# A hybrid decoder layer on one core: the stretch from the output projection to the T4 operand in a written-down engine order, and the first gate/up pair regrouped

## The chip, the cores and the metric

The kernel runs on one core of a Trainium2 chip. The metric is the time of one execution on the device, in microseconds. Each core has five engines that run their own instruction streams in order: TensorE (PE, matmuls and transposes), VectorE (DVE), ScalarE (ACT), GpSimd (POOL) and SyncE (SP, which here issues most DMA transfers).

## The reference

One decoder layer, 1024 positions by 1024 channels, float32:

```python
h = rms_norm(x, mix_norm_g[l])
proj = jnp.einsum('bsd,de->bse', h, w_in[l])
...
mixed = jnp.concatenate([fox_out, diff_out], axis=-1)   # 8 FoX heads, 4 diff heads
x = x + jnp.einsum('bse,ed->bsd', mixed, w_out[l])
h = rms_norm(x, ffn_norm_g[l])
g = jnp.einsum('bsd,df->bsf', h, w_gate[l])             # 1024 x 2816
u = jnp.einsum('bsd,df->bsf', h, w_up[l])
x = x + jnp.einsum('bsf,fd->bsd', jax.nn.silu(g) * u, w_down[l])
return rms_norm(x, final_norm_g)
```

## The kernel before

**Matmuls.** Every float32 product is made of three: each operand is split into a high part (cast on ScalarE) and a low part (source minus high part, a subtract on VectorE or GpSimd), and hi·hi, hi·lo and lo·hi are summed in PSUM. A name ending in `h` or `l` in a row is such a part.

**The norm loop.** After attention, `for n, tb in enumerate(order)` goes through the eight row blocks of 128 positions in the order 7, 6, 5, 4, 0, 1, 2, 3. A round n makes, for each of the two column halves, 12 matmuls of the second half of the output projection (`pso`, L601; its operands `mx` come from the last attention groups, `mix` L501, `mx` L506 and L507) and a residual add on VectorE (`x`, L796); then the row norm: Square with a sum on ScalarE (L134), a scale on VectorE (`ss`, L135), a power of -1/2 on GpSimd (`ss`, L136), and the multiply `xn` on VectorE (L801).

**The operands.** From round 2 on, a round also transposes the block of two rounds ago (`pt`, L753) and cuts it into operands of a seven-product (Strassen-Winograd) scheme. The product names are "11", "21", "T1" to "T4" and "22"; each has a high and a low tile of 512 positions. `second_half(t)`, for blocks 4 to 7, makes "22" (`h22h`, `h22l`), the kept halves `r12` and `r22`, and the difference T3 (`st`, L765). `first_half(t)`, for blocks 0 to 3, makes "11", the difference T1 (`st`, L775), updates `r22` with it on GpSimd (`r`, L776), and T2. `first_half_below(t)` makes "21" and the difference T4 (`st`, L786). Differences go through small tiles `st` of one pool.

**The weights.** Gate and up weights arrive as raw quarter blocks (`raw`, L715, two buffers), on SyncE's queue. The sums that the scheme needs are made on GpSimd (`st`, L723). The weight operands are `oh` (ScalarE, L708) and `ol` (VectorE, L709). Four of them, `early`, are made before and during the norm loop; their products "22" and "T3" of gate and up are held in PSUM. `strassen_first` makes the other five products of both matrices for pair 0: gate's "11" and "21", up's "11" and "21", then the rest (matmuls `pst`, L825). It loads both weights and makes the sums s1 and s2 again. Ten more pairs follow in `strassen`, then the down projection.

**Who sets the order.** A scheduler that simulates the program sets the order on each engine in this stretch; in the attention part and in the last part it is partly written down already (`tc.manual_schedule`: the engines named run their instructions in program order).

Of the kernel before, what the change touches and what calls it, by code (L numbers as in the profile page):

```python
# [18 lines left out]
P = 128  # L19
# [52 lines left out]
def layer(ctx: ExitStack, tc: tile.TileContext, x, mix_g, w_in, b_forget, lq1, lk1, lq2, lk2,  # L72
# [543 lines left out]
    def xa_half(tb, nh):  # L616
        return xa[tb][:, nh * 512:nh * 512 + 512]
# [94 lines left out]
    def raw_w(m, q, c0, n):  # L712
        raw = wp.tile([P, 1056], F32, tag="wr", name="raw")
        v = raw[:, :4 * n].rearrange("p (k c) -> p k c", k=4)
        nc.sync.dma_start(out=v, in_=w_gu[m][:, 4 * q:4 * q + 4, c0:c0 + n])  # L715
        return v

    def small():
        return fa.tile([P, 4, P], F32, tag="st", name="st")

    def w_sum(op, x, y):
        t = small()
        G.tensor_tensor(t, x, y, op)  # L723
        return t

    def w_blocks(m, pair):
        q0, q1 = (raw_w(m, q, 2 * pair * P, 2 * P) for q in range(2))
        return q0[:, :, 0:P], q0[:, :, P:2 * P], q1[:, :, 0:P], q1[:, :, P:2 * P]

    def early_operands(m):  # L730

        a11, a21, a12, a22 = w_blocks(m, 0)
        s2 = w_sum(ALU.subtract, w_sum(ALU.add, a21, a22), a11)
        return operand(w_sum(ALU.subtract, a12, s2)), operand(w_sum(ALU.subtract, a11, a21))

    early = [early_operands(m) for m in range(2)]
# [4 lines left out]
    def split_at(name, c, src, le):  # L741
        h, l = (x[:, :, c:c + P] for x in b_op[name])
        A.copy(h, src)
        le.tensor_tensor(l, src, h.bitcast(F32), ALU.subtract)

    turn = [0]

    def transposed(t, q):
        pool, tag = ((ps_p, "pj"), (ps_t, "t"))[turn[0] % 2]
# [30 lines left out]
    def first_half_below(t):  # L780

        c = t % 4 * P
        pv = transposed(t, 1)
        split_at("21", c, pv, V)
        t4 = small()
        V.tensor_sub(t4, pv, r22[:, :, c:c + P])  # L786
        split_at("T4", c, t4, V)

    order = (7, 6, 5, 4, 0, 1, 2, 3)
    for n, tb in enumerate(order):  # L790
        xt = x2[tb // 2][:, tb % 2]
# [10 lines left out]
        if n == 2:  # L802
            b_op["22"] = big("h22h"), big("h22l")
        if n == 6:
            for name in ("11", "T1", "T2"):
                b_op[name] = tuple(big(name + c) for c in "hl")
        if n >= 2:
            t = order[n - 2]
            (second_half if t >= 4 else first_half)(t)
    for t in (2, 3):  # L810
        first_half(t)
    for name in ("21", "T4"):
        b_op[name] = tuple(big(name + c) for c in "hl")

# [12 lines left out]
        return ps  # L827

    product.n = 0
    held = []  # L830
    for m in range(2):
        held.append([product(a, name, ((ps_s, "s"), (ps_s, "s"), (ps_s, "s"), (ps_p, "pj"))[2 * m + k])
                     for k, (a, name) in enumerate(zip(early[m], ("22", "T3")))])
        for t in range(2):
            first_half_below(2 * m + t)
# [66 lines left out]

    def strassen_first(takes):

        rest = []
        for m, take in enumerate(takes):
            a11, a21, a12, a22 = w_blocks(m, 0)
            p1, u2, u3 = kept_tiles()
            A.copy(p1, product(operand(a11), "11"))
            s1 = w_sum(ALU.add, a21, a22)  # L910
            s2 = w_sum(ALU.subtract, s1, a11)

            def finish(take=take, p1=p1, u2=u2, u3=u3, p3=held[m][0], p7=held[m][1], s1=s1, s2=s2,
                       a22=a22):
                ps5 = product(operand(s1), "T1")
                ps = product(operand(s2), "T2")
                V.tensor_add(u2, ps, p1)
                V.tensor_add(u3, p7, u2)
                take(1, 1, ps5, u3)
                V.tensor_add(u2, ps5, u2)  # L920
                take(0, 1, p3, u2)
                take(1, 0, product(operand(a22), "T4"), u3)

            take(0, 0, product(operand(a12), "21"), p1)
            rest.append(finish)
        for finish in rest:
            finish()

    for pair in range(NF // 2):
        me = V if pair == NF // 2 - 1 else G  # L930
# [251 lines left out]
```

## Time and profile before

| | |
|---|---|
| runs | 1267.75, 1268.8, 1270.53 us; median 1268.8 |
| profiled execution | 1264.56 us, of which the span on the engines is 1262.9 us |
| TensorE in the span | 1223.7 us (97%), granted clock 0.99 of full speed |
| stretch in question | about 567 to 660 us |

The profile is of one execution, with times from the span's start. An engine's row in a timeline shows its start, its duration and, in brackets, how long the engine stood idle before it and what ended that. Rows of matmuls overlap (the next starts before the one before has drained), so the pace is read from starts.

### The profile page before, as it was taken

What the parts mean: (1) busy time and instruction counts of PE and PEld (TensorE: products, weight loads), DVE (VectorE), ACT (ScalarE), POOL (GpSimd) and SP (SyncE); (2) the same over time, 40 slices, a digit from 0 to 9 for tenths busy, and PEclk for the clock granted to TensorE, in tenths of its full rate; (3) what the DMA queues carried; (4) which work ended last, traced back from release to release, by engine and by line L of the source; (5) the groups of instructions that cost most, each with busy time, mean ns of one, the idle gap of its engine ahead of it and who ended that gap; (6) DMA issues with size and microseconds to landing.
All of it is one profiled execution on the core that took longest, in us unless ns stands there. A gap on an engine that the chain in (4) does not pass through costs nothing.

```text
span 1262.9 us, 18429 instructions
## 1 busy us (share of the span) xinstructions
PE 1223.7 (97%) x6341; PEld 1041.5 (82%) x6341; DVE 865.1 (69%) x1625; ACT 571.2 (45%) x1209; POOL 718.3 (57%) x657
## 2 busy tenths in 40 slices
PE   8999999999999998999799999999999999999997
PEld 8889988987898887888578888888888887788886
DVE  6556766757786788877777566566565568868765
ACT  4345545646685665545533332233332245434424
POOL 2322333134204363235768877777787758999973
PEclk9999999999999999999899999999999999999999
DMA  6231223031202144033223333323333357735313
GB/s 218 65 109 43 68 73 85 26 98 45 51 8 80 51 142 180 9 138 100 94 82 108 107 119 109 108 80 105 101 109 125 100 190 236 217 117 183 97 55 133
DMA packets 93374, 131.42 MB, mean 104 GB/s; under 512 B 7585, under 2 KB 56289, under 8 KB 93281
## 3 DMA queue, kind: packets, MB, share of 16 engines
q1 hardware_dynamic: 91440, 124.22, 30.8%
q10 hardware_dynamic: 1840, 6.03, 1.3%
q8 instruction: 50, 0.82, 0.3%
q14 instruction: 44, 0.35, 0.1%
HBM read 93.75 MB, written 30.18 MB: 98 GB/s over the span
## 4 chain that ended last, share of the span: by engine, by line
PE 82%; POOL 6%; DVE 4%; issue 3%; DMA 3%; ACT 1%; SPq 0%; POOLq 0%; ACTq 0%; DVEq 0%
PE pst L825 32%; PE psd L1037 13%; PE psv L229 6%; PE pso L601 5%; PE pv L374 4%; PE tp L389 3%; PE s L329 2%; PE s L330 2%; POOL unit L1008 2%; POOL st L723 1%; PE psq_f1q L292 1%; PE psq_d2q L292 1%; PE psq_f2q L292 1%; PE psq_d3k L292 1%; PE psq_f1k L292 1%
## 5 line engine op out<-in xcount | busy, mean ns | idle before, releaser
L1037 PE MATMUL psd<-unit 128*128 128x512 f32 x924 | 212.1, 391 | 3.9 <-DVE x L1049 3.0
L1037 PEld LDWEIGHTS psd<-unit 128*128 128x128 f32 x924 | 174.2, 189 | 41.7 <-DVE x L1049 3.4
L709 DVE TENSOR_TENSOR ol<-st,oh 128x512 fp32r<-128x512 f32 x88 | 99.7, 1134 | 43.7 <-ACT oh L708 42.2
L1008 DVE TENSOR_TENSOR unit<-araw,unit 128x512 fp32r<-128x512 f32 x77 | 103.6, 1371 | 33.9 <-ACT unit L1007 20.3
L708 ACT CAST oh<-st 128x512 fp32r<-128x512 f32 x88 | 53.4, 619 | 152.8 <-POOL st L723 116.4
L333 ACT ACTIVATE pt<-pt,mn 128x896 f32<-128x896 f32 (+7 forms) x128 | 99.4, 777 | 41.8 <-DVE mn L331 39.9
L396 DVE TENSOR_TENSOR pl<-tp,ph 128x512 fp32r<-128x512 f32 (+1 forms) x120 | 75.2, 632 | 44.6 <-ACT ph L395 43.9
L395 ACT CAST ph<-tp 128x512 fp32r<-128x512 f32 (+1 forms) x120 | 64.1, 541 | 63.9 <-PE tp L389 54.1
L709 DVE TENSOR_TENSOR ol<-raw,oh 128x512 fp32r<-128x512 f32 x66 | 67.0, 1015 | 33.4 <-ACT oh L708 33.4
L723 POOL TENSOR_TENSOR st<-raw 128x512 f32<-128x512 f32 x46 | 59.9, 1302 | 41.6 <-DMA raw<-in_w_gate_dram 22.6
L939 POOL TENSOR_TENSOR sg<-sg,cc 128x512 f32<-128x512 f32 x44 | 65.6, 1493 | 29.8 <-ACT sg L938 26.0
L1007 ACT CAST unit<-araw 128x512 fp32r<-128x512 f32 x77 | 47.4, 619 | 74.9 <-PE psd L1037 34.0
L421 POOL TENSOR_SCALAR_AFFINE_SELECT cb<-cb 128x128 f32<-128x128 f32 x64 | 22.0, 345 | 99.1 <-DVE mn L331 60.1
L708 ACT CAST oh<-raw 128x512 fp32r<-128x512 f32 x66 | 40.8, 618 | 81.5 <-PE pst L825 71.5
L945 POOL TENSOR_TENSOR sg<-sg,cc 128x512 f32<-128x512 f32 x40 | 58.9, 1476 | 30.2 <-DVE cc L944 30.1
L393 POOL MEMSET ph<- 128x128 f32 x48 | 9.9, 205 | 106.9 <-PE pv L374 100.7
L389 PE MATMUL tp<-ident,pt 128*128 128x128 f32 x432 | 67.3, 274 | 0.4 <-DVE pl L396 0.3
L126 POOL TENSOR_TENSOR wl<-wr,wh 128x1024 fp32r<-128x1024 f32 x26 | 62.8, 2415 | 1.4
L125 POOL TENSOR_SCALAR wh<-wr 128x1024 fp32r<-128x1024 f32 x26 | 29.6, 1139 | 52.6 <-PE psq_f2k L292 13.1
L389 PEld LDWEIGHTS tp<-ident,pt 128*128 128x128 f32 x432 | 51.4, 141 | 5.4 <-DVE pl L396 1.4
L229 PE MATMUL psv<-wh,hh 128*128 128x256 f32 x192 | 55.0, 287 | 0.1
L229 PE MATMUL psv<-wl,hh 128*128 128x256 f32 x192 | 54.7, 285 | 0.0
(381 smaller groups left out, 3838.7 us busy)
## 6 DMA issues: line engine op xcount, KB each, us to landing
araw<-act_d SPq DMA_DIRECT2D x77, 256.0 KB, 2.6
raw<-in_w_gate_dram SPq DMA_DIRECT2D x24, 512.0 KB, 3.6
raw<-in_w_up_dram SPq DMA_DIRECT2D x24, 512.0 KB, 3.9
wr<-in_w_in_dram SPq DMA_DIRECT2D x22, 512.0 KB, 4.0
act_d<-sa SPq DMA_DIRECT2D x44, 256.0 KB, 2.2
wraw<-in_w_down_dram SPq DMA_DIRECT2D x40, 256.0 KB, 4.4
act_d<-sg SPq DMA_DIRECT2D x33, 256.0 KB, 2.0
xt<-in_x_dram SPq DMA_DIRECT2D x8, 512.0 KB, 5.4
```

Of the source, the lines that this page charges most:

```text
L229: T.matmul(ps[:, :n], hslice(l, dt, tb), r, start=(k == 0), stop=(k == 23))
L333: A.activation(pt[:, :L], pt[:, :L], AF.Exp, bias=mn[:, nb - 1:nb], scale=-1.0, accum_out=mn[:, 2:3])
L389: T.transpose(tp[:, a * 256 + b * P:a * 256 + (b + 1) * P], pts[b][:, sb * P:(sb + 1) * P], ident)
L395: A.copy(ph[:, o:], tp[:, o:])
L396: V.tensor_sub(pl[:, o:], tp[:, o:], ph[:, o:].bitcast(F32))
L708: A.copy(h, src)
L709: V.tensor_sub(l, src, h.bitcast(F32))
L723: G.tensor_tensor(t, x, y, op)
L825: T.matmul(ps, l[:, j], r[:, j], start=(k == 0), stop=(k == 11))
L939: G.tensor_mul(sg, sg, g)
L1008: lo = le.tensor_tensor(u[:, 2 * k + 1], src, u[:, 2 * k].bitcast(F32), ALU.subtract)
L1037: T.matmul(open_banks[i, m], l, r, start=(k == 0 and not top), stop=(k == last), skip_group_check=top)
```

## The change

Five things. The norm loop, the operands after it and the four held products run in program order on TensorE, VectorE, ScalarE and GpSimd, and the program's text is rewritten to fit. The differences T3, T1, T4 and the early weight sums share one tile `temps` of two halves. The early weight sums are made one step per round (`plan`) and kept, so that `strassen_first` doesn't make s1 and s2 again (four GpSimd sums fewer); it does gate's five products, then up's. Gate's raw weights are loaded again in round 6. And the two reloads of the residual (`x2r`, 1 MB each) go from ScalarE's queue after pair 0 to SyncE's queue behind the last weight load of pairs 2 and 3.

```diff
+NORM_MAN = {EngineType.PE, EngineType.DVE, EngineType.Activation, EngineType.Pool}
...
+    temps = bp.tile([P, 2, 512], F32, tag="b", name="temps")
...
+    def second_half(t, pvs):
+        A.copy(at(r12, t), pvs[0])
+        hi_part("22", t, pvs[1])
+        A.copy(at(r22, t), pvs[1])
+        V.tensor_sub(temp(0), pvs[1], at(r12, t))
+        lo_part("22", t, pvs[1], V)
+        hi_part("T3", t, temp(0))
+        return lambda: lo_part("T3", t, temp(0), G)
+    def first_half(t, pvs):
+        hi_part("11", t, pvs[0])
+        V.tensor_sub(temp(0), at(r12, t), pvs[0])
+        lo_part("11", t, pvs[0], V)
+        hi_part("T1", t, temp(0))
+        def pool():
+            G.tensor_sub(at(r22, t), at(r22, t), temp(0))
+            lo_part("T1", t, temp(0), G)
+            hi_part("T2", t, at(r22, t))
+        return pool
...
+    plan = {0: (0, 0), 1: (0, 1), 2: (0, 2), 3: (1, 0), 4: (1, 1), 5: (1, 2)}
     order = (7, 6, 5, 4, 0, 1, 2, 3)
+    manual = tc.manual_schedule(engines=NORM_MAN)
+    manual.__enter__()
     for n, tb in enumerate(order):
...
             out_matmuls((4, 5, 6, 7), w2[nh], tb, ps)
+            if nh == 0 and n >= 2:
+                t = order[n - 2]
+                pvs = [transposed(t, q) for q in range(2 if t >= 4 else 1)]
             V.tensor_add(xt[:, cs], ps, xa_half(tb, nh))
+            if nh == 0 and n >= 2:
+                late = (second_half if t >= 4 else first_half)(t, pvs)
+            if nh == 0 and plan.get(n - 1, (0, 0))[1]:
+                early[plan[n - 1][0]].append(operand(temp(1)))
         xns[tb] = pp.tile([P, D], F32, tag="p", name="xn")
         r = rstd_of(xt, xns[tb], sm)
         V.scalar_tensor_tensor(xns[tb], xt, r, gb2, ALU.mult, ALU.mult)
...
+        if n >= 2:
+            late()
+        if n in plan:
+            early_sum(*plan[n])
...
+    held[0][0] = product(early[0][0], "22", SS)
+    pvs = [transposed(2, 0)]
+    first_half(2, pvs)()
+    held[0][1] = product(early[0][1], "T3", SS)
+    pvs = [transposed(3, 0)]
+    first_half(3, pvs)()
+    a_first = [operand(w_first[0][0])]
+    for t in range(4):
+        lo_part("T2", t, at(r22, t), G)
+    held[1][0] = product(early[1][0], "22", SS)
...
+    manual.__exit__(None, None, None)
...
     def x2_load(h):
-        nc.scalar.dma_start(out=x2[h], in_=x2_d[(2 * h - 4) * P:(2 * h - 2) * P, :]
-                            .rearrange("(b p) d -> p b d", p=P))
+        with tc.issue_after(raw_w.last.ins):
+            nc.sync.dma_start(out=x2[h], in_=x2_d[(2 * h - 4) * P:(2 * h - 2) * P, :]
+                              .rearrange("(b p) d -> p b d", p=P))
```

Where the order moves, in three places. First a round of the norm loop on VectorE. Before, with the rounds of two blocks (tiles `x_6402` and `x_6296`) interleaved:

```order
L135 TENSOR_SCALAR ss<-ss 128x1
L801 SCALAR_TENSOR_TENSOR xn<-x_6402,ss,gb_6787 128x1024
L796 TENSOR_TENSOR x_6402<-pso,x_6402 128x512
L709 TENSOR_TENSOR ol<-st,oh 128x512
L796 TENSOR_TENSOR x_6402<-pso,x_6402 128x512
L765 TENSOR_TENSOR st<-pt,r_6835 128x512
L135 TENSOR_SCALAR ss<-ss 128x1
L765 TENSOR_TENSOR st<-pt,r_6835 128x512
L796 TENSOR_TENSOR x_6296<-pso,x_6296 128x512
L709 TENSOR_TENSOR ol<-st,oh 128x512
L801 SCALAR_TENSOR_TENSOR xn<-x_6402,ss,gb_6787 128x1024
L709 TENSOR_TENSOR ol<-st,oh 128x512
```

After, round 5, whose tiles are `x_6402`, and the first add of round 6:

```order
L830 SCALAR_TENSOR_TENSOR xn<-x_6402,ss,gb_6787 128x1024
L823 TENSOR_TENSOR x_6402<-pso,x_6402 128x512
L765 TENSOR_TENSOR temps<-pt,r_6795 128x512
L748 TENSOR_TENSOR h22l<-pt,h22h 128x4x128
L710 TENSOR_TENSOR ol<-temps,oh 128x512
L823 TENSOR_TENSOR x_6402<-pso,x_6402 128x512
L136 TENSOR_SCALAR ss<-ss 128x1
L830 SCALAR_TENSOR_TENSOR xn<-x_6402,ss,gb_6787 128x1024
L823 TENSOR_TENSOR x_6296<-pso,x_6296 128x512
```

Before, a residual add or two stands ahead of each `xn` and the weight operands' `ol` fill the places between; now each round runs through before the next begins: add, difference, low part, `ol`, add, scale, `xn`.

Second, the start of the loop, on TensorE, where `rp` (a transpose that spreads the last attention groups' reciprocals, L499 before, L500 after) leads to `mix` and `mx` on VectorE. Before, both instructions of the last group's `rp` stood together, near the end of round 3's matmuls:

```order
L601 MATMUL pso<-w2h,mx_5962 128x512
L601 MATMUL pso<-w2h,mx_5958 128x512
L499 MATMUL rp<-ident,dg 128x128 x2
L753 MATMUL pt<-ident,xn 128x128 x4
L601 MATMUL pso<-w2l,mx_5958 128x512
```

After, they are taken apart: one stands among round 2's transposes, the other behind the end of round 2's second half (`w2h`, `w2l`) and three matmuls of round 3:

```order
L602 MATMUL pso<-w2l,mx_5958 128x512
L602 MATMUL pso<-w2h,mx_5962 128x512
L602 MATMUL pso<-wh,mx_5958 128x512
L602 MATMUL pso<-wl,mx_5958 128x512
L602 MATMUL pso<-wh,mx_5962 128x512
L500 MATMUL rp<-ident,dg 128x128
```

And on VectorE, the instructions that need it and those behind them (after):

```order
L502 SCALAR_TENSOR_TENSOR mix<-o,g_777,rp 128x256
L494 TENSOR_SCALAR dg<-ones,rr 128x128 x2
L508 TENSOR_TENSOR mx_5960<-mix,mx_5956 128x256
L502 SCALAR_TENSOR_TENSOR mix<-o,g_777,rp 128x256
L508 TENSOR_TENSOR mx_5960<-mix,mx_5956 128x256
L830 SCALAR_TENSOR_TENSOR xn<-x_6011,ss,gb_6787 128x1024
L823 TENSOR_TENSOR x_6092<-pso,x_6092 128x512
L765 TENSOR_TENSOR temps<-pt,r_6795 128x512
```

The multiply `xn` of round 1 (tile `x_6011`), the first add of round 2 and all behind it now stand behind the second `mix` and `mx`, which need that `rp`; before, the `xn` of round 1 stood ahead of the first `mix`, and that of round 2 ahead of the second.

Third, the end of the loop on VectorE, where the low parts and differences of the last blocks are made. Before:

```order
L744 TENSOR_TENSOR 11l<-pt,11h 128x4x128
L775 TENSOR_TENSOR st<-r_6835,pt 128x512
L786 TENSOR_TENSOR st<-pt,r_6836 128x512
L744 TENSOR_TENSOR 21l<-pt,21h 128x4x128
L786 TENSOR_TENSOR st<-pt,r_6836 128x512
L744 TENSOR_TENSOR T4l<-st,T4h 128x4x128
L744 TENSOR_TENSOR 21l<-pt,21h 128x4x128 x2
L786 TENSOR_TENSOR st<-pt,r_6836 128x512 x2
L709 TENSOR_TENSOR ol<-raw,oh 128x512
L744 TENSOR_TENSOR T4l<-st,T4h 128x4x128
```

After:

```order
L774 TENSOR_TENSOR temps<-r_6795,pt 128x512
L748 TENSOR_TENSOR 11l<-pt,11h 128x4x128
L710 TENSOR_TENSOR ol<-raw,oh 128x512
L788 TENSOR_TENSOR temps<-pt,r_6796 128x512
L748 TENSOR_TENSOR 21l<-pt,21h 128x4x128
L748 TENSOR_TENSOR T4l<-temps,T4h 128x4x128
L788 TENSOR_TENSOR temps<-pt,r_6796 128x512
L748 TENSOR_TENSOR 21l<-pt,21h 128x4x128
L748 TENSOR_TENSOR T4l<-temps,T4h 128x4x128
L710 TENSOR_TENSOR ol<-raw,oh 128x512
```

The first low part of gate's weights (`ol<-raw`) now stands ahead of all four T4 differences instead of behind them, and each difference goes through a half of `temps`. What it waits for there is on GpSimd (after):

```order
L137 TENSOR_TENSOR ss<-ss,mhalf 128x1
L779 TENSOR_TENSOR r_6796<-r_6796,temps 128x4x128
L748 TENSOR_TENSOR T1l<-temps,T1h 128x4x128
L137 TENSOR_TENSOR ss<-ss,mhalf 128x1
L779 TENSOR_TENSOR r_6796<-r_6796,temps 128x4x128
L748 TENSOR_TENSOR T1l<-temps,T1h 128x4x128
L779 TENSOR_TENSOR r_6796<-r_6796,temps 128x4x128
```

Each T1l reads the same half of `temps` that the next block's difference writes, and behind the power of a round (`ss`) stand an update of `r22` and a T1l.

## Rows read from the trace of the kernel before

**Rows 1.** The page: the span, and part 1, busy time of each engine with its share of the span and its number of instructions.

```profile
span 1262.9 us, 18429 instructions
PE 1223.7 (97%) x6341; PEld 1041.5 (82%) x6341; DVE 865.1 (69%) x1625; ACT 571.2 (45%) x1209; POOL 718.3 (57%) x657
```

**Rows 2.** The table by windows: three stretches, from late in the norm loop to the first products of gate. For each the window, its length, then for each engine busy time and instructions in it, the granted TensorE clock as a share of full speed, the DMA engines' busy share and what they moved.

```profile
552.00:600.00 48.00, 47.80 (x244) 39.65 (x242) 33.86 (x59) 20.85 (x41) 20.50 (x20) 1.00 0.32 110
600.00:622.00 22.00, 15.71 (x79) 12.71 (x79) 18.07 (x27) 13.32 (x25) 19.16 (x15) 0.90 0.15 49
622.00:632.00 10.00, 6.50 (x24) 4.95 (x23) 6.38 (x6) 3.38 (x6) 4.50 (x3) 0.84 0.61 206
```

**Rows 3.** The waits of TensorE from 545 to 1040 us, the longest five: line that waited, what for, microseconds in all, times, longest.

```profile
PE pst L825 <- DVE st L786: 3.6, 1, 3.6
PE pst L825 <- ACT oh L708: 3.5, 1, 3.5
PE pt L753 <- DVE st L775: 2.4, 1, 2.4
PE pst L825 <- DVE cc L937: 0.9, 1, 0.9
PE pst L825 <- DVE kept L917: 0.8, 1, 0.8
```

**Rows 4.** The timeline of TensorE: start, duration, line, operation, output and inputs, number of instructions merged in the row, and in brackets the idle time just before and what ended it. From the last matmul of round 2's output projection to the last product of pair 0.

```profile
567.03 0.48 PE L601 MATMUL pso<-w2h,mx 128*128 128x512 f32 x1
598.98 0.39 PE L601 MATMUL pso<-w2h,mx 128*128 128x512 f32 x1
620.92 0.77 PE L825 MATMUL pst<-11h,oh 128*128 128x512 f32 x1 [3.65 <-DVE st L786]
621.49 0.63 PE L825 MATMUL pst<-11l,oh 128*128 128x512 f32 x1
631.77 0.79 PE L825 MATMUL pst<-11h,oh 128*128 128x512 f32 x1 [3.50 <-ACT oh L708]
654.86 0.39 PE L825 MATMUL pst<-T4h,ol 128*128 128x512 f32 x1
```

**Rows 5.** The timelines of VectorE, ScalarE and GpSimd: one row normalised, from its second residual add over Square and power to the multiply by the reciprocal root, and the instruction after it on VectorE.

```profile
597.18 0.68 DVE L796 TENSOR_TENSOR x<-pso,x 128x512 f32<-128x512 f32 x1
597.89 1.06 ACT L134 ACTIVATE xn<-x 128x1024 f32<-128x1024 f32 x1 [3.53 <-DVE x L796]
599.31 0.54 POOL L136 TENSOR_TENSOR ss<-ss,mhalf 128x1 f32<-128x1 f32 x1 [2.60 <-DVE ss L135]
600.15 1.28 DVE L801 SCALAR_TENSOR_TENSOR xn<-x,ss,gb 128x1024 f32<-128x1024 f32 x1
601.35 0.68 DVE L765 TENSOR_TENSOR st<-pt,r 128x512 f32<-128x512 f32 x1
```

**Rows 6.** The same timelines, another row's multiply with GpSimd at work beside it.

```profile
576.87 0.55 POOL L136 TENSOR_TENSOR ss<-ss,mhalf 128x1 f32<-128x1 f32 x1 [4.67 <-DVE ss L135]
577.39 1.29 POOL L723 TENSOR_TENSOR st<-st,raw 128x512 f32<-128x512 f32 x1
578.75 2.16 POOL L723 TENSOR_TENSOR st<-raw,st 128x512 f32<-128x512 f32 x1
577.45 2.31 DVE L801 SCALAR_TENSOR_TENSOR xn<-x,ss,gb 128x1024 f32<-128x1024 f32 x1 [0.67 <-POOL ss L136]
```

**Rows 7.** The same timelines: a difference, its cast, a weight operand's cast, and elsewhere a residual add with a weight operand's low part behind it; last, such a low part beside GpSimd's T3l.

```profile
591.41 0.69 DVE L765 TENSOR_TENSOR st<-pt,r 128x512 f32<-128x512 f32 x1 [0.62 <-POOL st L723]
592.14 0.62 ACT L743 CAST T3h<-st 128x512 fp32r<-128x512 f32 x1
592.67 0.62 ACT L708 CAST oh<-st 128x512 fp32r<-128x512 f32 x1
584.80 0.68 DVE L796 TENSOR_TENSOR x<-pso,x 128x512 f32<-128x512 f32 x1
585.40 0.68 DVE L709 TENSOR_TENSOR ol<-st,oh 128x512 fp32r<-128x512 f32 x1
595.48 1.78 DVE L709 TENSOR_TENSOR ol<-st,oh 128x512 fp32r<-128x512 f32 x1
```

**Rows 8.** VectorE and ScalarE: the last attention group's mix, its cast and its low part.

```profile
573.45 0.48 DVE L501 SCALAR_TENSOR_TENSOR mix<-o,g,rp 128x256 f32<-128x256 f32 x1 [0.17 <-PE rp L499]
574.36 0.41 ACT L506 CAST mx<-mix 128x256 fp32r<-128x256 f32 x1
575.56 0.42 DVE L507 TENSOR_TENSOR mx<-mix,mx 128x256 fp32r<-128x256 f32 x1
```

**Rows 9.** GpSimd (two of each merged) and one low part of T4 on VectorE.

```profile
609.99 3.52 POOL L776 TENSOR_TENSOR r<-r,st 128x512 f32<-128x512 f32 x2
613.48 2.48 POOL L744 TENSOR_TENSOR T1l<-st,T1h 128x512 fp32r<-128x512 f32 x2
617.68 1.30 DVE L744 TENSOR_TENSOR T4l<-st,T4h 128x512 fp32r<-128x512 f32 x1
```

**Rows 10.** The table of windows for a stretch inside the attention part in which TensorE idled.

```profile
480.00:493.00 13.00, 8.77 (x60) 7.37 (x59) 11.37 (x31) 8.73 (x25) 6.60 (x12) 1.00 0.87 321
```

**Rows 11.** The DMA issues, the residual reload's row: tiles, queue, how many, size of each, median microseconds from issue to landing; and a row of SyncE's timeline, two gate weight issues merged.

```profile
x2r<-x_d ACTq DMA_DIRECT2D x2, 1024.0 KB, 4.8
745.28 9.63 SPq L715 DMA_DIRECT2D raw<-in_w_gate_dram  x2
```

More of the change, by code (lines that the diff above doesn't have):

```diff
@@ L714, in raw_w @@
         v = raw[:, :4 * n].rearrange("p (k c) -> p k c", k=4)
-        nc.sync.dma_start(out=v, in_=w_gu[m][:, 4 * q:4 * q + 4, c0:c0 + n])
+        raw_w.last = nc.sync.dma_start(out=v, in_=w_gu[m][:, 4 * q:4 * q + 4, c0:c0 + n])
         return v
@@ L739, in layer, with temp, at, hi_part @@
     b_op["T3"] = tuple(fa.tile([P, 4, 512], F32R, tag="xb", name="T3" + c) for c in "hl")
[L741 to L744, printed above, removed]
+    temps = bp.tile([P, 2, 512], F32, tag="b", name="temps")
+    def temp(k):
+        return temps[:, k].rearrange("p (j t) -> p j t", j=4)
+    def at(x, t):
+        c = t % 4 * P
+        return x[:, :, c:c + P]
+    def hi_part(name, t, src):
+        A.copy(at(b_op[name][0], t), src)
+    def lo_part(name, t, src, e):
+        h, l = (at(x, t) for x in b_op[name])
+        e.tensor_tensor(l, src, h.bitcast(F32), ALU.subtract)
     turn = [0]
-    def transposed(t, q):
-        pool, tag = ((ps_p, "pj"), (ps_t, "t"))[turn[0] % 2]
+    def transposed(t, q, banks=((ps_p, "pj"), (ps_t, "t"))):
+        pool, tag = banks[turn[0] % len(banks)]
         turn[0] += 1
@@ new lines, in layer, with early_sum @@
+    w_first, w_sums, early = {}, {}, [[], []]
+    def early_sum(m, k):
+        if k == 0:
+            w_first[m] = w_blocks(m, 0)
+        a11, a21, a12, a22 = w_first[m]
+        if k == 0:
+            s1 = w_sum(ALU.add, a21, a22)
+            w_sums[m] = s1, w_sum(ALU.subtract, s1, a11)
+        elif k == 1:
+            G.tensor_tensor(temp(1), a12, w_sums[m][1], ALU.subtract)
+        else:
+            G.tensor_tensor(temp(1), a11, a21, ALU.subtract)
+    plan = {0: (0, 0), 1: (0, 1), 2: (0, 2), 3: (1, 0), 4: (1, 1), 5: (1, 2)}
@@ L801, in layer @@
         V.scalar_tensor_tensor(xns[tb], xt, r, gb2, ALU.mult, ALU.mult)
-        if n == 2:
+        if tb >= 4:
+            nc.scalar.dma_start(out=x2_d[(tb - 4) * P:(tb - 3) * P, :], in_=xt)
+        if n >= 2:
+            late()
+        if n in plan:
+            early_sum(*plan[n])
+        if n == 1:
             b_op["22"] = big("h22h"), big("h22l")
         if n == 6:
+            w_first[0] = w_blocks(0, 0)
+        if n == 5:
             for name in ("11", "T1", "T2"):
                 b_op[name] = tuple(big(name + c) for c in "hl")
[L807 to L813, printed above, removed]
     def product(a, name, at=None):
@@ L829, in layer @@
     product.n = 0
[L830 to L835, printed above, removed]
+    SS, PJ, TT = (ps_s, "s"), (ps_p, "pj"), (ps_t, "t")
+    held = [[None, None], [None, None]]
+    for name in ("21", "T4"):
+        b_op[name] = tuple(big(name + c) for c in "hl")
+    held[0][0] = product(early[0][0], "22", SS)
[8 more added lines that the diff above has]
+    held[1][0] = product(early[1][0], "22", SS)
+    pvs = [transposed(t, 1) for t in (0, 1)]
+    for t in (0, 1):
+        first_half_below(t, pvs[t])
+    held[1][1] = product(early[1][1], "T3", PJ)
+    pvs = [transposed(t, 1, (TT, TT, PJ)) for t in (2, 3)]
+    a_first.append(operand(w_first[0][2]))
+    for t in (2, 3):
+        first_half_below(t, pvs[t - 2])
+    manual.__exit__(None, None, None)
     norms.close()
@@ L903, in strassen_first @@
     def strassen_first(takes):
-        rest = []
         for m, take in enumerate(takes):
-            a11, a21, a12, a22 = w_blocks(m, 0)
+            a11, a21, a12, a22 = w_blocks(m, 0) if m else w_first[0]
+            s1, s2 = w_sums[m]
             p1, u2, u3 = kept_tiles()
[L909 to L927, printed above, removed]
+            A.copy(p1, product(a_first[0] if m == 0 else operand(a11), "11"))
+            take(0, 0, product(a_first[1] if m == 0 else operand(a12), "21"), p1)
+            ps5 = product(operand(s1), "T1")
+            ps = product(operand(s2), "T2")
+            V.tensor_add(u2, ps, p1)
+            V.tensor_add(u3, held[m][1], u2)
+            take(1, 1, ps5, u3)
+            V.tensor_add(u2, ps5, u2)
+            take(0, 1, held[m][0], u2)
+            take(1, 0, product(operand(a22), "T4"), u3)
     for pair in range(NF // 2):
```

45 lines of the change are left out of this document (9 added, 36 removed).

## The prediction

> **What bounds the kernel now.** The page first: TensorE is busy 1223.7 of 1262.9 us [rows 1], so only its idle time and its slow matmuls can be won, and anything that makes it idle longer is lost. The windows show where it idles in the stretch that changes: not in the norm loop (47.80 of 48.00 us busy, granted clock 1.00), but in the 32 us behind it, 15.71 of 22 and 6.50 of 10 us, at 0.90 and 0.84 [rows 2]. The waits name five causes [rows 3]: 2.4 us for a T1 difference, 3.6 us ahead of gate's "11" (its PSUM bank is freed by a T4 difference), 3.5 us for up's first weight operand, then 0.9 and 0.8 us at the start of pair 1. After each of the longest two the first matmuls run at the lower level of the clock, 1.2 instead of 2.4 GHz: 0.63 us instead of 0.39 [rows 4]. From start to start that is about 0.20 more; eight such after 620.92 cost 1.6 us, six or seven after 631.77 cost 1.3.
>
> So the loop is paced by TensorE: the last matmul of round 2 starts at 567.03, that of round 7 at 598.98 [rows 4], five rounds in 31.95 us, 6.4 us each. VectorE, busy 33.86 of 48 us there [rows 2], has slack because the scheduler interleaves two rounds.
>
> **The loop after the change.** VectorE's order now holds `xn(n)` ahead of the next round's first add, and nothing between. The chain of a round, from the trace of before:
>
> 1. From the end of the second add (597.18 + 0.68 = 597.86) over Square, scale and power, which ends at 599.85 (599.31 + 0.54) [rows 5]. In [rows 6] `xn` starts 0.03 us behind the power's end (577.42, 577.45). Together 2.0 us.
> 2. `xn` itself. With GpSimd idle it takes 1.28 us and the next instruction starts 1.20 us after it [rows 5]; with GpSimd's sums beside it 2.31 us [rows 6], so the next after 2.23. GpSimd's T3l, or the update of `r22`, now stands directly behind the power in every round from 2 on, so I take 2.23.
> 3. First add to difference 0.60 us (the spacing at 584.80 and 585.40 [rows 7]). Difference to `ol`: 0.69 us, the T3h cast at 592.14, the `oh` cast at 592.67 with 0.62 us [rows 7], 1.9 us from the difference's start; the low part of "22" or "11" fits inside. `ol` to second add 0.60, that add 0.68.
>
> That is 2.0 + 2.23 + 0.6 + 1.9 + 0.6 + 0.68 = 8.0 us. Rounds 4 and 7 make no weight operand: a low part of 0.6 us stands in the place of the 1.9, 6.7 us. Both are above TensorE's 6.4, so VectorE's chain becomes the bound and TensorE waits for free PSUM banks.
>
> In step 2 the slow `xn` and the GpSimd sum that follows it (2.16 us instead of 1.29) show an exclusive use in turn. The Trainium skill, "SBUF — State Buffer", section "Who interferes with whom", says it so: a VectorE instruction with two SBUF inputs contends with a GpSimd one that reads SBUF, and whoever issues first holds the shared ports to its end. By that rule the two would take 1.29 + 1.28 = 2.57 us, 0.26 more than the row, or 1.3 us more over five rounds; the trace agrees in kind and I use its row.
>
> Start of the chain. TensorE's work up to the split `rp` is what ended at 567.35 before (567.03 and a step of 0.32), plus eight transposes that stand ahead now (0.85), one `rp` and three matmuls (1.0), plus 1.2 us for idle places early in the loop where before filler matmuls stood (an estimate: five steps of 0.23; bounds 0 and 3): 570.6. Behind it `mix` 0.48, the `mx` cast 0.41 and its low part 0.42 [rows 8]: 572.0. Then `xn` of round 1 with GpSimd idle, 1.2; the first add of round 2 at 573.2, and by step 3 the end of its second add is 0.6 + 1.9 + 0.6 + 0.68 later, 577.0. Rounds 3, 5 and 6 add 24.0, rounds 4 and 7 13.4 and about 0.5 more in round 7, whose difference waits for a T1l to free its half of `temps`: 614.9.
>
> **The tail.** From there to "11". Power 2.0; update of `r22` and T1l for block 1 beside `xn`, 1.76 + 1.24 = 3.0 (half of each pair in [rows 9]); then, since one half of `temps` serves blocks 2 and 3, the steps alternate: difference 0.7, GpSimd's two steps 2.5, difference 0.7, update 1.25, cast of T2 0.53, cast of the weights 0.62. That is 11.3. On VectorE then follow `ol` 0.9 beside GpSimd, and twice a T4 difference 0.6, 21l 0.6 and T4l with its cast 1.4 (1.30 alone in [rows 9]), then `ol` 0.7, and the difference and 21l of block 2 that free the bank, 1.3: 8.1. "11" starts at 614.9 + 11.3 + 8.1 = 634.3, where before it starts at 620.92 [rows 4]: 13.4 us later.
>
> **What comes back.** From "11" on, before takes until 655.25 (654.86 + 0.39 [rows 4]) for the remaining 120 matmuls, 34.3 us, with the wait of 3.50 and two slow starts. Its last 96 start 23.09 us apart, first to last [rows 4]; without the 1.3 of the slow start that is 0.229 us each. Now gate's 60 matmuls run before up needs weights, up's load (whose buffer is free once gate's "11" operand is made) lands under them, and 120 matmuls at 0.229 us with one slow start of 1.6 take 29.1. That gives back 5.2. Of the 1.7 us at the start of pair 1 I take half, 0.8, since T1 and T4 of up are no longer the last.
>
> **At nothing.** The four GpSimd sums, 1.3 us each as in [rows 6], are off the path once "11" has started. Gate's reload in round 6 has the rest of the loop to land. The residual reloads land in 4.8 us [rows 11] on SyncE's queue; the next weight issue stands some 9 us off (two issues span 9.63 us, [rows 11]); without that cover each could cost up to 4.8. The instructions of the loop get no slower clock: idle places of this size left it at 1.00 where TensorE was busy 8.77 of 13 us [rows 10].
>
> **Sum.** 13.4 - 5.2 - 0.8 = +7.4, so 1272.0 us against the profiled 1264.56, which lies 4.2 us under the median of 1268.8; on the median **1276 us**. About 2.5 us (0.2%) is what a measurement can tell from no change.
>
> **The rivals.**
>
> *Slower is wrong, faster (chance 0.18).* The loop stays paced by TensorE: the chain of a round comes to 6.4 us or less, because GpSimd's low parts miss `xn`, or casts start earlier. For it: without contention step 2 is 1.2, and the rounds come to 7.0 and 5.7, 32.4 us for the five, next to TensorE's 32; VectorE's share of 33.86 in 48 us. Against it: the two contended rows and the fixed order. Then round 7 ends at 570.4 + 32 = 602.4, "11" starts 19.4 later at 621.8, the 120 matmuls end at 650.9, 4.4 under before; with the 0.8, 1268.8 - 5.2 = 1263.6. It decides where "11" starts before 626.9 (620.92 + 5.2 + 0.8). If the tail too is free of contention, four to seven more, 1257. The Trainium skill, "Perfetto Trace Analysis", section "Identifying the Most-Contended Engine", looks for the most contended engine by its busy share, for TensorE by that of its weight loads; by that TensorE, with 39.65 of 48 us against VectorE's 33.86 [rows 2], would go on setting the loop's pace, as in this rival. The trace of before agrees for the old order; for the new one it cannot tell, since a busy share shows a load and not the length of a chain.
>
> *No change (0.12).* The chain bounds the loop but without contention: five rounds lose 1.03 each, the tail about 1.7, so "11" starts at 627.4 and the total moves by +0.5: 1269.3. The gain from up's weights then just pays for the tail.
>
> *Slower (0.70)*, of which my own range is 1271.5 to 1283. Its lower end has half the contention. Its upper end has each `ol` contended in turn (1.78 instead of 0.68 [rows 7], four of them 4.4 us), no gain at pair 1 (0.8), and one more slow start (1.3): 1282, and a little for the start's bound.
>
> The range is 1263 to 1283: at the low side it reaches the faster rival's likelier price, at the high side the bounds above; what is left out is the freest tail and the reload without cover.
>
> **What would show it.** In the profile of the changed kernel: the second adds of rounds 2 to 7 about 8, 6.7, 8, 8 and 6.7 us apart; `xn` at 2.2 to 2.3 us with a GpSimd instruction starting beside it; TensorE's last `pso` near 610, with waits for PSUM in the loop; "11" near 634; no wait for up's `raw`; TensorE's idle time from 545 to 665 longer by some 7 us. Wrong, if rounds come 6.4 us apart, if `xn` stays at 1.28, or if "11" starts before 627. The waits at pair 1 and the reloads show in pairs 1 to 3, where nothing else should move.

## The result, and the profile after

The changed kernel takes 1282.57 us (median of 4 runs, 1281.52 to 1285.43) against 1268.8 for the kernel before: 1.0111 times, with a 95% interval of 1.009 to 1.0132. That is 13.8 us slower, where 7.4 were forecast; it lies at the upper edge of the range. The profiled executions are 1281.52 and 1264.56 us, 17.0 apart, because the profiled one of before lies 4.2 us under its median and that of after 1.05 under its own. The page and the windows of the changed kernel:

```profile
span 1279.8 us, 18426 instructions
PE 1230.0 (96%) x6341; PEld 1043.5 (82%) x6341; DVE 865.0 (68%) x1625; ACT 572.2 (45%) x1209; POOL 715.0 (56%) x653
```

```profile
545.00:567.00 22.00, 19.75 (x108) 17.10 (x107) 13.91 (x39) 8.72 (x24) 7.34 (x13) 0.92 0.36 120
567.00:600.00 33.00, 28.53 (x142) 22.71 (x142) 20.81 (x30) 14.13 (x27) 15.87 (x14) 1.00 0.23 80
600.00:622.00 22.00, 18.23 (x79) 13.07 (x78) 15.22 (x20) 7.94 (x14) 10.81 (x8) 1.00 0.17 48
622.00:640.00 18.00, 10.51 (x44) 8.42 (x44) 11.97 (x14) 7.98 (x15) 14.90 (x11) 0.79 0.10 30
640.00:680.00 40.00, 36.18 (x147) 29.04 (x148) 24.72 (x35) 15.89 (x28) 17.88 (x14) 0.92 0.25 73
```

The columns are those of [rows 2]. Work per engine is nearly what it was ([rows 1]), with four GpSimd instructions fewer. TensorE now idles in the loop, too: from 567 to 600 us it is busy 28.53 of 33 us, where before it was 32.80. The stretch from 622 to 640 us is no better than before (10.51 of 18 us; 14.50 before). Its waits from 545 to 1060 us:

```profile
PE pt L757 <- DVE xn L830: 10.2, 7, 3.8
PE pst L855 <- ACT T4h L744: 3.6, 1, 3.6
PE pt L757 <- DVE 21l L748: 2.2, 1, 2.2
PE sp L489 <- DVE mix L502: 1.6, 1, 1.6
PE rp L500 <- DVE dg L494: 1.6, 2, 1.0
PE pst L855 <- DVE cc L976: 1.5, 1, 1.5
```

Up's weights, 3.5 us in [rows 3], are gone from the list; ten microseconds of transposes that wait for `xn` have come. No wait of the output projection (`pso`) for a free PSUM bank is in it. One round on VectorE and GpSimd, and the second adds of the rounds after it (VectorE's timeline; round 2's add first):

```profile
581.81 0.68 DVE L823 TENSOR_TENSOR x<-pso,x 128x512 f32<-128x512 f32 x1
584.54 2.30 DVE L830 SCALAR_TENSOR_TENSOR xn<-x,ss,gb 128x1024 f32<-128x1024 f32 x1 [0.68 <-POOL ss L137]
584.47 1.29 POOL L748 TENSOR_TENSOR T3l<-temps,T3h 128x512 fp32r<-128x512 f32 x1
585.71 2.26 POOL L807 TENSOR_TENSOR temps<-raw 128x512 f32<-128x512 f32 x1
589.85 0.68 DVE L823 TENSOR_TENSOR x<-pso,x 128x512 f32<-128x512 f32 x1
596.60 0.68 DVE L823 TENSOR_TENSOR x<-pso,x 128x512 f32<-128x512 f32 x1
604.62 0.68 DVE L823 TENSOR_TENSOR x<-pso,x 128x512 f32<-128x512 f32 x1
612.66 0.68 DVE L823 TENSOR_TENSOR x<-pso,x 128x512 f32<-128x512 f32 x1
620.06 0.68 DVE L823 TENSOR_TENSOR x<-pso,x 128x512 f32<-128x512 f32 x1
```

The rounds are 8.04, 6.75, 8.02, 8.04 and 7.40 us long; forecast were 8.0, 6.7, 8.0, 8.0 and 7.2. Every `xn` from round 2 on has T3l or the update of `r22` starting 0.07 us ahead of it and takes 2.28 to 2.31 us.

The start of the chain, on TensorE and VectorE (`sp` sums the squares of an attention group's output, `dg` holds the reciprocal roots made of it, `rp` transposes them):

```profile
553.53 0.75 PE L489 MATMUL sp<-ones,dg 128*128 128x1 f32 x4 [1.65 <-DVE mix L502]
571.87 0.30 PE L500 MATMUL rp<-ident,dg 128*128 128x128 f32 x1 [1.03 <-DVE dg L494]
575.90 0.27 PE L500 MATMUL rp<-ident,dg 128*128 128x128 f32 x1
576.21 0.48 DVE L502 SCALAR_TENSOR_TENSOR mix<-o,g,rp 128x256 f32<-128x256 f32 x1 [2.86 <-PE rp L500]
577.17 0.42 DVE L508 TENSOR_TENSOR mx<-mix,mx 128x256 fp32r<-128x256 f32 x1 [0.47 <-ACT mx L507]
577.51 1.28 DVE L830 SCALAR_TENSOR_TENSOR xn<-x,ss,gb 128x1024 f32<-128x1024 f32 x1
```

VectorE stands idle for 2.86 us until the split-off `rp` comes, with `xn` of round 1 queued behind it. In the kernel before, the second adds of round 2 and of round 7 are these rows of VectorE's timeline:

```profile
567.55 0.69 DVE L796 TENSOR_TENSOR x<-pso,x 128x512 f32<-128x512 f32 x1 [0.18 <-PE pso L601]
603.74 0.68 DVE L796 TENSOR_TENSOR x<-pso,x 128x512 f32<-128x512 f32 x1
```

By ends, round 2 is 14.25 us late (582.49 against 568.24) and round 7 is 16.3 late (620.74 against 604.42). So most of the lag is there when the chain begins; the rounds themselves add 2.1.

The tail and the first pair, on VectorE and TensorE:

```profile
629.56 0.69 DVE L774 TENSOR_TENSOR temps<-r,pt 128x512 f32<-128x512 f32 x1 [2.04 <-POOL T1l L748]
632.82 1.83 DVE L710 TENSOR_TENSOR ol<-raw,oh 128x512 fp32r<-128x512 f32 x1 [1.98 <-ACT oh L709]
635.94 1.63 DVE L748 TENSOR_TENSOR T4l<-temps,T4h 128x512 fp32r<-128x512 f32 x1
641.49 0.76 PE L855 MATMUL pst<-11h,oh 128*128 128x512 f32 x1 [3.56 <-ACT T4h L744]
667.67 0.50 PE L855 MATMUL pst<-21h,oh 128*128 128x512 f32 x1 [1.55 <-DVE cc L976]
676.51 0.50 PE L855 MATMUL pst<-11h,oh 128*128 128x512 f32 x1 [0.79 <-DVE kept L961]
```

Gate's "11" starts 20.6 us later than in [rows 4], pair 1's "11" 16.6 later (before: 659.91). Behind that point the kernels run alike to the end; the spans differ by 16.9.

### The profile page after: what moved, and what is told of

It reads as the page before. It is cut to its first block, busy times and chain, and to the rows that moved or that the text cites. A ratio compares the mean times of both kernels' runs of the same rounds, so it can differ in the third digit from the quotient of the medians.

```text
span 1279.8 us, 18426 instructions
## 1 busy us (share of the span) xinstructions
PE 1230.0 (96%) x6341; PEld 1043.5 (82%) x6341; DVE 865.0 (68%) x1625; ACT 572.2 (45%) x1209; POOL 715.0 (56%) x653
## 4 chain that ended last, share of the span: by engine, by line
PE 79%; POOL 7%; DVE 5%; issue 4%; ACT 2%; DMA 2%; SPq 0%; POOLq 0%; ACTq 0%; DVEq 0%
PE pst L855 31%; PE psd L1076 13%; PE psv L230 6%; PE pv L375 4%; PE pso L602 3%; PE tp L390 3%; PE s L330 2%; PE s L331 2%; POOL unit L1047 1%; PE psq_f1q L293 1%; PE psq_d2q L293 1%; PE psq_f2q L293 1%; PE psq_d3k L293 1%; PE psq_f1k L293 1%; PE psq_f3q L293 1%
## 5 line engine op out<-in xcount | busy, mean ns | idle before, releaser
L710 DVE TENSOR_TENSOR ol<-st,oh 128x512 fp32r<-128x512 f32 x84 | 90.7, 1081 | 50.4 <-ACT oh L709 49.1
L724 POOL TENSOR_TENSOR st<-raw 128x512 f32<-128x512 f32 x42 | 55.4, 1320 | 31.9 <-DMA raw<-in_w_gate_dram 23.0
```

The source lines that it names most:

```text
L710: V.tensor_sub(l, src, h.bitcast(F32))
```

## The experiments

Ratios are to the kernel before, run on the same chip beside each group; intervals are 95%. Where only a part of the code is shown, the rest is the changed kernel.

### The written order taken out

```diff
-    manual = tc.manual_schedule(engines=NORM_MAN)
-    manual.__enter__()
...
-    manual.__exit__(None, None, None)
```

> The changed kernel with the written-down order taken out: the scheduler orders the same program (one temps tile, kept sums, gate first, reloads behind the weights). Theory A (VectorE's written chain, with GpSimd beside xn, paces the loop and delays the end of it): the scheduler interleaves the rounds again, second adds come 6 to 6.5 us apart, round 7's second add ends near 605 instead of 620.7, and the time falls to 1265 to 1271. Rival B (the loss comes from the regrouped first pair, the shared temps tile or the moved reloads, not from the order): the time stays above 1278.

Measured: 1267.89 us, 0.9988 (0.9978 to 0.9998). All of the loss is the order's. The second add of round 7 ends at 606.41 us, 14.3 sooner than in the changed kernel. What is left of the change is worth little: the interval just excludes no change, and this version is the fastest of all that were run, ahead of both kernels. TensorE from 545 to 600 us is again full:

```profile
545.00:580.00 35.00, 34.63 (x194) 29.51 (x194) 24.95 (x60) 15.13 (x37) 14.94 (x21) 1.00 0.33 118
580.00:600.00 20.00, 20.00 (x101) 16.66 (x100) 14.65 (x19) 10.66 (x19) 13.87 (x12) 1.00 0.29 84
```

### The norm chain half a round later

`power` holds the scale and the power of the round before, `multiply` its `xn`:

```diff
+            if nh == 1 and n >= 1:
+                multiply()
             V.tensor_add(xt[:, cs], ps, xa_half(tb, nh))
+            if nh == 0 and n >= 1:
+                power()
...
-        r = rstd_of(xt, xns[tb], sm)
-        V.scalar_tensor_tensor(xns[tb], xt, r, gb2, ALU.mult, ALU.mult)
+        A.activation(xns[tb], xt, AF.Square, accum_out=ss[:, 0:1])
```

> The changed kernel with the order still written down, but the scale, the power and the multiply xn of a round put one half-round later, behind the next round's first add, difference and low part; nothing else moves. Theory A: the 2.0 us from second add to xn leave VectorE's chain, which comes to about 6 us a round beside GpSimd, so TensorE paces the rounds at 6.4 us; round 7's second add comes 6 to 9 us earlier than in the changed kernel and the tail stays: 1274 to 1277. Rival C (a written order as such is at fault, because any fixed order waits somewhere): rounds stay at 7.5 to 8 us, 1281 or more. Rival B: no change, 1282.

Measured: 1282.38 us, 1.0107 (1.0091 to 1.0123): no gain. The time is that of rival C, but the rounds did get shorter: the second adds of rounds 2 and 7 are 35.6 us apart (581.65 and 617.28) instead of 38.25, where theory A wanted some 32. The 2.0 us left VectorE's chain and another wait took part of their place. From TensorE, ScalarE and VectorE:

```profile
574.06 1.97 PE L757 MATMUL pt<-ident,xn 128*128 128x128 f32 x8 [4.20 <-DVE xn L841]
591.18 1.06 ACT L834 ACTIVATE xn<-x 128x1024 f32<-128x1024 f32 x1 [4.26 <-DVE x L825]
592.24 0.56 ACT L762 COPY r<-pt 128x512 f32<-128x512 f32 x1
593.19 0.60 ACT L764 COPY r<-pt 128x512 f32<-128x512 f32 x1
593.87 0.69 DVE L765 TENSOR_TENSOR temps<-pt,r 128x512 f32<-128x512 f32 x1 [1.35 <-ACT r L764]
```

ScalarE's order puts the copies of the transposes behind the round's Square, so the difference now waits for Square and three copies (the second of them is not shown). What the rounds gain is spent elsewhere. `xn` of round 0 now stands behind the last `mx` too, so TensorE waits 4.20 us at the start, with a clock of 0.74 from 567 to 580 us. And gate's "11" starts at 636.48, 5.0 us sooner than in the changed kernel (2.4 of them are there at 545 us already), but pair 1's "11" comes 37.8 us behind it instead of 35.0.

### GpSimd's low parts and differences as zeros

```diff
-        return lambda: lo_part("T3", t, temp(0), G)
+        return lambda: G.memset(at(b_op["T3"][1], t).bitcast(F32), 0.0)
...
-            lo_part("T1", t, temp(0), G)
+            G.memset(at(b_op["T1"][1], t).bitcast(F32), 0.0)
...
-            G.tensor_tensor(temp(1), a12, w_sums[m][1], ALU.subtract)
+            G.memset(temp(1), 0.0)
...
-            G.tensor_tensor(temp(1), a11, a21, ALU.subtract)
+            G.memset(temp(1), 0.0)
```

> The changed kernel with GpSimd's low parts of T3 and T1 and the four early weight differences written as zeros (a fill that reads nothing) instead of subtracted; the update of r22 stays. So that part of the products is left out. Theory A, contention: xn beside a fill takes 1.28 us instead of 2.30 in rounds 2 to 5, and still 2.3 in rounds 6 and 7, where the update stands beside it; rounds with a weight operand come 7.0 us apart instead of 8.0; with T1l gone from the tail about 8 us in all, near 1274. Rival (xn is slow for another reason, or the fill holds it up as well): xn stays at 2.3, rounds at 8.0, and only the tail gains 2 to 3 us: 1279 to 1280.

Measured: 1275.67 us, 1.0066 (1.0043 to 1.0088), 6.9 less than the changed kernel. From GpSimd and VectorE, `xn` of round 2 beside two fills, and that of round 6 beside the update of `r22`, which starts at 609.14:

```profile
582.35 0.53 POOL L768 MEMSET T3l<- 128x512 f32 x1
582.81 0.53 POOL L807 MEMSET temps<- 128x512 f32 x1
582.44 1.29 DVE L830 SCALAR_TENSOR_TENSOR xn<-x,ss,gb 128x1024 f32<-128x1024 f32 x1 [0.67 <-POOL ss L137]
609.21 2.30 DVE L830 SCALAR_TENSOR_TENSOR xn<-x,ss,gb 128x1024 f32<-128x1024 f32 x1 [0.67 <-POOL ss L137]
```

The price of the contention is as it was expected: 1.01 us a round (7.03 between second adds instead of 8.04). The two fills cover 0.9 us of this `xn`, and it keeps its 1.29. So the difference lies between a GpSimd instruction that reads and one that only writes. The Trainium skill, "SBUF — State Buffer", section "Who interferes with whom", states just that for a VectorE instruction with two SBUF inputs, and the trace agrees: 1.29 us beside the fills, 2.30 beside the update.

### Two buffers for the last T1 differences

```diff
+    t1s = wp.tile([P, 1024], F32, tag="wh", name="t1s")
+    t1 = [t1s[:, 512 * k:512 * k + 512].rearrange("p (j t) -> p j t", j=4) for k in range(2)]
-    first_half(2, pvs)()
+    first_half(2, pvs, t1[0])()
...
-    first_half(3, pvs)()
+    first_half(3, pvs, t1[1])()
```

> The changed kernel with the T1 differences of the last two blocks in two buffers of their own instead of one half of temps. Theory A: they no longer wait for T1l; from the end of round 7's second add to gate's 11 the profile shows 19.0 us instead of 20.7, all else the same. Rival (GpSimd's chain alone sets the tail): 20.5 or more.

A single run, so without an interval: 1284.13 us. From the end of round 7's second add (621.43) to gate's "11" (641.23) it is 19.8 us instead of 20.75, half of what was expected. The next wait appears where that for T1l was (VectorE, then ScalarE):

```profile
629.29 0.69 DVE L774 TENSOR_TENSOR t1s<-r,pt 128x512 f32<-128x512 f32 x1 [2.16 <-ACT 11h L744]
628.15 0.62 ACT L744 CAST T2h<-r 128x512 fp32r<-128x512 f32 x1 [0.97 <-POOL r L779]
628.67 0.58 ACT L744 CAST 11h<-pt 128x512 fp32r<-128x512 f32 x1
```

The difference of block 3 now waits for ScalarE's `11h`, which stands behind `T2h` of block 2, and that waits for GpSimd's update of `r22`. So GpSimd's chain still sets this step, by way of ScalarE's order. The same edit together with that of the first experiment, without the written order:

> The kernel without the written order, with the T1 differences of the last two blocks in buffers of their own. Theory A3 (with the scheduler free, what is left of the tail's waits, 4.6 us and 1.7 us of TensorE for low parts on VectorE behind a temps difference, comes from the single half of temps): 2 to 4 us faster than without the written order alone, 1264 to 1266. Rival (GpSimd's chain of update and T1l sets them anyway): the same as without the order, 1267 to 1269.

Measured: 1269.11 us, 1.0000 (0.9988 to 1.0012), so nothing gained; the rival holds, and the waits moved to other instructions.

### The order from round 2, from round 4, or behind the loop only

The diff of the first of the three; the second has `n == 4`:

```diff
-    manual = tc.manual_schedule(engines=NORM_MAN)
-    manual.__enter__()
     for n, tb in enumerate(order):
+        if n == 2:
+            manual = tc.manual_schedule(engines=NORM_MAN)
+            manual.__enter__()
```

> The changed kernel with the written-down order beginning at round 2 instead of round 0; rounds 0 and 1, beside the last attention groups, go back to the scheduler. Theory A2 (part of the loss lies ahead of the chain: without the freedom to fill, TensorE idles and falls to its lower clock between 545 and 580 us, busy 31.1 of 35 us at 0.95 there, against 34.7 at 1.00 before): TensorE is busy 33 us or more in that window, the second add of round 2 ends 3 to 4 us earlier than 582.5, rounds stay at 8.0 and 6.7, and the time falls by 3 to 4: 1278 to 1280. Rival (the start is free, the chain from round 2 makes all of it): within 1 us of the changed kernel, 1282.

Measured: 1285.25 us, 1.0118 (1.0103 to 1.0133). Theory A2 falls: TensorE is busy 31.47 of 35 us from 545 to 580, and an `rp` waits 3.2 us for its `dg`; the difference of round 2 now stands behind the last `mx` in place of `xn`, and VectorE waits 5.23 us for the second `rp`. The rival asked for a time within 1 us of the changed kernel; the medians are 2.7 us apart, but each interval contains the other's ratio.

> The changed kernel with the written-down order beginning at round 4. Two theories for where the loop loses. S (start): in the changed kernel round 2's second add ends 14.3 us later than before (582.49 against 568.23), and rounds 2 to 7 then take 38.3 us against 36.2; so nearly all of it lies at the start, where all of VectorE's work from round 2 on stands behind the last attention group's second mx. With the scheduler free until round 3, the adds of rounds 2 and 3 slip ahead of it, the written rounds 4 to 7 keep their 6.7 to 8 us, and the time falls to 1270 to 1275. P (pace): the rounds' own length is the loss, four of five slow rounds remain, and the time stays at 1279 or more.

Measured: 1277.82 us, 1.0066 (1.0048 to 1.0084): between the two theories, so neither is whole. VectorE's first and second add of round 4, `xn` of round 4 and the second add of round 7:

```profile
581.00 0.69 DVE L824 TENSOR_TENSOR x<-pso,x 128x512 f32<-128x512 f32 x1 [0.93 <-PE pso L602]
587.94 0.67 DVE L824 TENSOR_TENSOR x<-pso,x 128x512 f32<-128x512 f32 x1
592.92 2.29 DVE L831 SCALAR_TENSOR_TENSOR xn<-x,ss,gb 128x1024 f32<-128x1024 f32 x1 [2.94 <-POOL ss L137]
613.65 0.68 DVE L824 TENSOR_TENSOR x<-pso,x 128x512 f32<-128x512 f32 x1
```

With the scheduler free, round 4 begins on VectorE within 0.7 us of before (580.28). Then, where the written order sets in, 6.3 us pass between the first add's end and the second's start (differences and low parts of two blocks stand between them), `xn` waits 2.94 us for its power, and the following rounds are 10.3, 8.0 and 7.4 us long: round 7's second add ends 9.9 us later than in the kernel before. This execution was already 3.0 us late at 545 us (see the part that the kernels share, below), so 6.9 of it are the loop's.

With the order behind the loop only (entered ahead of the held products):

> The changed kernel with the written-down order only behind the loop (the last two blocks, the held products, 21 and T4), the loop itself left to the scheduler. Theory A: the rounds come at TensorE's pace again, round 7's second add ends within 2 us of 606; the tail from there to gate's 11 stays near 20.7 us, 4.2 more than before; what the regrouped pair gives back, 4.0, pays for it: 1268 to 1272. Rival (the tail's order is the larger loss): 1275 or more.

Measured: 1271.58 us, 1.0021 (1.0010 to 1.0031). Against the version without any order that is some 4 us for the tail; the other 11 of the 14.7 belong to the loop. Gate's "11" starts at 624.95, 20.6 us behind round 7's second add (604.34), as in the changed kernel.

### The reloads back on ScalarE's queue

```diff
-        with tc.issue_after(raw_w.last.ins):
-            nc.sync.dma_start(out=x2[h], in_=x2_d[(2 * h - 4) * P:(2 * h - 2) * P, :]
+        nc.scalar.dma_start(out=x2[h], in_=x2_d[(2 * h - 4) * P:(2 * h - 2) * P, :]
...
-        if pair in (2, 3):
-            x2_load(pair)
+        if pair == 0:
+            x2_load(2)
+            x2_load(3)
```

> The changed kernel with the residual reloads back on ScalarE's queue behind pair 0. Theory A (they are hidden in both places): within 1.5 us of the changed kernel's 1282.6, although the reload takes 8.4 us from issue to landing on SyncE's queue instead of 4.8. Rival (1 MB behind the weights delays the next pair's weights by up to 4.8 us each): 1278 or less.

Measured: 1281.95 us, 1.0098 (1.0084 to 1.0111): no difference. Theory A holds; the reload is hidden in both places.

### The order without VectorE, and on VectorE alone

```diff
-NORM_MAN = {EngineType.PE, EngineType.DVE, EngineType.Activation, EngineType.Pool}
+NORM_MAN = {EngineType.PE, EngineType.Activation, EngineType.Pool}
```

> The changed kernel with the written-down order kept on TensorE, ScalarE and GpSimd and taken from VectorE. If VectorE's order is what costs: 1268 to 1273, TensorE's waits for xn (10.2 us) fall under 5. If the order on TensorE (transposes ahead of the second half, the split rp) or on GpSimd costs as much: 1277 or more.

Measured: 1277.22 us, 1.0060 (1.0041 to 1.0078).

```diff
+NORM_MAN = {EngineType.DVE}
```

> The counterpart: the written-down order on VectorE alone, the other three engines left to the scheduler. If VectorE's order is what costs: 1279 to 1284. If the loss needs the other engines' order beside it: 1275 or less.

Measured: 1275.95 us, 1.0055 (1.0038 to 1.0071). So either half of the order costs 8 to 9 us over the version without it, and both together 14.7. VectorE's order is not the one cause: without it, the order of TensorE holds the split `rp` and the idle places ahead of it (31.30 of 35 us busy from 545 to 580, clock 0.95, as in the changed kernel); alone, it makes TensorE's output projection wait for an add:

```profile
PE pso L602 <- DVE x L823: 4.2, 1, 4.2
```

### Gate's five products first, in the kernel before

```diff
             take(0, 0, product(operand(a12), "21"), p1)
-            rest.append(finish)
-        for finish in rest:
-            finish()
+            finish()
```

> The kernel before with one part of the change: the first pair makes gate's five products, then up's five (sums still made twice, the scheduler's order, reloads on ScalarE's queue). Theory (what the changed kernel gives back behind gate's 11 comes from up's weights landing under gate's products): the wait of 3.50 us and its slow start fall, 1265 to 1267. Rival (the sums s1 and s2 that gate's T1 and T2 now need first are made by GpSimd no sooner, so another wait takes its place): within 1 us of before.

Measured: 1271.42 us, 1.0023 (1.0008 to 1.0037), slower. The wait for up's weights goes and one as long comes behind it (TensorE):

```profile
652.76 0.50 PE L825 MATMUL pst<-T2h,oh 128*128 128x512 f32 x1 [3.68 <-ACT oh L708]
```

So the regrouping alone does not pay in the kernel before. Whether the kept sums or the earlier loads make it pay in the changed kernel was not tried.

## Why the prediction was right, and where its sizes were off

The direction, the chain of a round and of the tail, and what comes back in kind were right; 13.8 us stood where 7.4 were forecast. That this lies in the range is in part luck: the upper end was made of contended `ol`s, no gain at pair 1 and one more slow start, while most of the excess came from the start of the loop and from a part that was in no term. By the profiled executions' 17.0 us the time would lie above the range. Term by term, on the profiled executions, where pair 1's "11" is 16.6 us late and the sum said 7.4:

- **A part that the kernels share** (+1.7, not in the sum). Near 545 us the same matmul `s`, of the attention part, starts at 546.39 instead of 544.69, although TensorE's instructions ahead of it, back to 400 us, are, as far as they are recorded, the same in the same order. The windows of before and after, in this order, show the clock:

```profile
480.00:490.00 10.00, 7.61 (x54) 6.37 (x52) 8.37 (x24) 8.73 (x25) 6.32 (x11) 1.00 0.82 299
480.00:490.00 10.00, 7.27 (x42) 6.67 (x43) 8.07 (x24) 6.83 (x22) 6.31 (x10) 0.83 0.91 358
```

  In the traces of the experiments this matmul starts between 544.02 and 547.71, so the part varies from execution to execution. It can be a part of the 3.2 us by which the profiles differ more than the medians; that is not shown.
- **The start** (forecast 577.0 for the end of round 2's second add, measured 582.49; 3.8 us besides the part above). The term of 1.2 us for idle places was mis-sized: `sp` waited 1.65 us for `mix`, `rp` 0.6 and 1.03 for `dg`, and behind the first the clock fell (0.92 from 545 to 567 us; about 1.7 us by the starts from 553.53 to 557.17). That makes 5.0, above the bound of 3 that the prediction set. (Its terms up to `rp` add up to 570.4, where it writes 570.6.) With that, the sentence that the loop gets no slower clock was wrong at its start, where [rows 10] was a bad witness; it held from 567 to 622.
- **The rounds** (37.9 forecast, 38.25 measured): right, each to 0.2 us, and the third experiment shows the contention in them. What TensorE waits for in them was named wrongly: not free PSUM banks, but `xn` itself, which its transposes read (10.2 us in the loop and the tail, 5.1 of them by 615 us).
- **The tail** (19.4 forecast, 20.75 measured): right in its steps. The update and T1l beside `xn` took 3.5 us instead of 3.0, `ol` 1.83 instead of 0.9 and the first T4l 1.63, both beside GpSimd; the second T4l, 0.69 alone, gave some of it back.
- **What comes back** (6.0 forecast, 4.0 measured: from gate's "11" to pair 1's "11" 38.99 us before, 35.02 after). Up's weights did land under gate's products. But the waits at pair 1 grew to 1.55 + 0.79 where half of 1.7 was to go, and the slow start was ten matmuls instead of eight.

1.7 + 3.8 + 0.35 + 1.35 + 2.0 = 9.2, the difference of 16.6 and 7.4.

One reading in the text was wrong though its numbers were not. It set VectorE's new rounds of 8.0 and 6.7 us against TensorE's 6.4 and called that the loss. VectorE's own five rounds took 36.2 us before (568.24 to 604.42), since it was falling behind TensorE; so the longer rounds cost 2.1, and the sum's 577.0 already held 8.8 us of lag against 568.24, which the text never compared. The experiments bear this out in part: freeing the start up to round 4 gains 4.8 us, freeing the whole loop 11.0. That a lag forms again where the written order begins is shown for its beginning at round 2 and at round 4; how the 11 us divide between start and rounds is not settled, since each engine's half of the order costs 8 to 9 alone.

The two rivals fell. The faster one needed 32 us for rounds 3 to 7; the written ones took 38.25, and without most of the contention, in the third experiment, 33.5 (second adds at 579.71 and 613.23). Its mechanism, a loop paced by TensorE, is what the first experiment shows with the scheduler's order, and so the rule of the Trainium skill that stands beside it ("Perfetto Trace Analysis", section "Identifying the Most-Contended Engine") names the bound of the old order and not of the new one: from 567 to 600 us TensorE's weight loads are busy 22.71 us against VectorE's 20.81, and yet TensorE waits for VectorE's `xn`. The rival without change needed a tail and loop free of contention; `xn` at 2.30 rules it out. At nothing stood the reloads (right, by the experiment on them), gate's reload in round 6 (no wait for it shows) and the four sums (the version without the order, with those sums gone, is 0.12% under before, so they and the rest of the change are worth about 1.5 us).

## What to carry to other kernels

When an order written by hand replaces a scheduler's, price the chain that the in-order engine now has to run through, and compare the time at which it starts, not only its pace, with the same point of the old trace. Look for instructions of the stage before that end up ahead of the new stage's first ones: here a split transpose 3 us late held back a whole engine's queue. Loosening the order of one side alone gave back 5 to 7 of the 14.7 us, and taking out a single wait nothing, because another fixed order stood right behind it.

## What the runs showed of the hardware

GpSimd fills of 128x512 (0.53 us each) beside VectorE's multiply with two SBUF inputs leave it at 1.29 us, where a GpSimd subtract makes it 2.30; the subtract itself keeps its 1.29, and the one behind it takes 2.26. A 1 MB reload took 8.4 us from issue to landing on SyncE's queue, issued 0.5 us behind a weight load, and 4.8 on ScalarE's, with no difference in the kernel's time. And from 480 to 490 us, with TensorE busy 7.61 and 7.27 of 10 us, its clock was 1.00 in one execution and 0.83 in the other, with its instructions in the same order.
